# A hybrid encoder block with 16 experts: the router's sort cut into two runs of 64, stored rows without the norm's weight, and products without use behind the first gather

## Chip, cores and metric

The kernel runs on one core of one Trainium2 chip. The metric is the device time of one execution in microseconds (us), as the median of several runs. A profile of one execution, with the start, length and waits of every instruction, stands beside it. The engines go by these names: PE is TensorE (products), PEld its weight loads, DVE VectorE, ACT ScalarE, POOL GpSimd, SP SyncE (here a queue that issues DMAs).

## What is computed

One encoder layer over 1024 tokens of width 1024, all in float32. The part in question lies between the two halves of the layer: the output projection of the mixers, the router, and the first expert.

```
x = x + einsum('bsd,de->bse', mixed, w_out)          # output projection
h2 = rms_norm(x, norm_ffn_g)                         # x * rsqrt(mean(x*x) + eps) * norm_ffn_g
aff = softmax(h2 @ w_router)                         # 1024 tokens x 16 experts
g, idx = top_k(aff.T, 128)                           # each expert takes its 128 best tokens
xs = h2[idx]                                         # rows of each expert
y = (silu(xs @ w_gate) * (xs @ w_up)) @ w_down       # d_ff 2048
x = x + scatter_add(y * g, idx);  out = rms_norm(x, final_norm_g)
```

## The kernel before, in words

Products run in split precision: a float32 matrix is cut into a high part (`whi`, one ACT copy, L105) and the rest (`wlo`, one DVE subtraction, L106), and three products of 128x512 stand for one. Weights come in pieces of 128x1024 (512 KB each). `load` (L91) issues a piece's DMA on SP, `split` (L100) makes its two parts, `stream` (L118) runs splits `MSA` = 3 pieces and loads up to `ROOM` slots ahead of the piece in use. Nothing is reordered: each engine runs its instructions in the order in which the program names them, and only semaphores hold them.

**Output projection and router, L844 to L895.** For each of 8 token tiles `t` of 128 rows, `out_k` (L790) makes 6 products for each of 8 slices `k`; the last tile is made in two halves of 512 columns. The sum is added to `X2[t]` on DVE (L859, for the last tile L873 and L880). Between the products of tile t the program places the router's work for tile t-1:

- `route_a` (L798): 8 PE transposes of the rows, an ACT copy to `xT`, an ACT `Square` with a row sum into the scratch tile `h2`, `rstd_of` (L167: two DVE steps and an ACT `Sqrt`), then on POOL two products over 128x1024 (L818 by the inverse norm, L819 by the norm's weight `gfb`) and the DMA of the rows to `h2_d` (L820).
- `logits` (L824): 8 small products with the router's weights `wr`, which hold the norm's weight already.
- `route_b` (L831): softmax: a DVE maximum (L834), a DVE product (L835), ACT `Exp` (L836), and on DVE a reciprocal (L838) and a scaling (L839).

**The threshold.** An expert's 128 best tokens are those above the 128th largest of its 1024 values. `sort_steps` (L713) turns one or two tiles of values (PE, L718), copies them with a sign to `row` (L720) and sorts 128 values per expert by 16 times `max` (8 largest, L725) with `match_replace` (L729) between them. `merge_steps` (L734) joins a sorted tile with the best 128 so far: one elementwise maximum of a rising and a falling list (L743), then 7 levels of pairwise `max` and `min` (L750, L752) that sort the result again. These chains are Python generators. `bg(n)` (L767) runs the next n steps, taking the open sort and merge in turn; `BGN`, `BG7`, `T1` to `T3` say how many steps go at each place. After the last tile's softmax the sort of tile 7 starts (L888) and the loop at L889 runs all steps that are left.

**From threshold to the first expert.** `theta` (L891) is turned (L898), compared with all values (L902, L903); prefix sums by products (L905 to L917) give each chosen token its place; four DVE steps (L918 to L921) cut the values into three bfloat16 parts in `aux`. `prep(e)` (L934) builds one-hot rows `oh`, `gather(e)` (L939) gets token numbers and weights by 8 small products `pa` and issues the indirect DMA that fetches expert e's 128 rows from `h2_d` (L951). `xst(e)` (L955) turns those rows in two halves of four transposes, each with one ACT copy to `xh` (L964, 128x512) and one DVE subtraction to `xl` (L965). Then `gu` (L970) and `down` (L999) run for 16 experts with 4 quarters each; `xst(e+1)` is placed in quarters 2 and 3 of expert e (L1078, L1079). Ahead of expert 0 the order is `prep(0)`, `gather(0)`, two splits (`SA0` = 1), `xst(0)` (L1066 to L1069).

Of the kernel before, what the change touches and what calls it, by code (L numbers as in the profile page):

```python
# [8 lines left out]
F32 = mybir.dt.float32  # L9
# [3 lines left out]
AF = mybir.ActivationFunctionType  # L13
# [12 lines left out]
MSA, ROOM, ROOM0, PF0, PF1, SA0 = 3, 36, 43, 9, 15, 1  # L26
WOS = (0, 0, 0, 0, 0, 1, 2, 3)
FY = 4
BGN, BG7, T1, T2, T3 = 4, 3, 2, 2, 4
LAG = 2  # L30
FILL = (5, 2, 1, 1) + (1, 0, 1, 0) * 7 + (1, 1, 1, 1, 1)

# [9 lines left out]
def f32(ap):  # L42
    return ap.bitcast(F32)
# [3 lines left out]
def block_kernel(ctx, tc, x, wpre, wexp, cols, rows, sguw, out):  # L47
    nc = tc.nc
# [11 lines left out]
    def slot(shape, dt, name):  # L60
        return big.tile(shape, dt, name=name, tag="s", bufs=NSLOT)
# [10 lines left out]
    def psml(name, shape=(128, 512)):  # L72
        return psp.tile(list(shape), F32, name=name, tag="t", bufs=2)
# [90 lines left out]
    def bcast_row(t, lo_, n):  # L164
        nc.gpsimd.dma_start(t, bass.AP(tensor=rows.tensor, offset=rows.offset + lo_, ap=[[0, 128], [1, n]]))
# [540 lines left out]
    nc.vector.memset(affw, 0.0)  # L706
    aff = affw[:, :, 0:16]
    theta = cst.tile([16, 1], F32, name="theta")
    sgn = cst.tile([64, 1], F32, name="sgn")
    nc.vector.memset(sgn, -1.0)  # L710
    nc.vector.memset(sgn[0:32], 1.0)

    def sort_steps(t, n):  # L713


        rows_ = 16 + 32 * (n - 1)
        pt = psml("paT", (32 * n, 128))
# [4 lines left out]
        dst = srp.tile([64, 128], F32, name="srt", bufs=3)  # L722
        for r in range(16):
            yield
            nc.vector.max(dst[:rows_, 8 * r:8 * r + 8], cur[:rows_])  # L725
            if r < 15:
                yield
                nx = srp.tile([64, 128], F32, name="srw", bufs=4)
                nc.vector.match_replace(nx[:rows_], dst[:rows_, 8 * r:8 * r + 8], cur[:rows_], -3.0e38)  # L729
                cur = nx  # L730
        for j in range(n):
            SRT[t + j] = dst[32 * j:32 * j + 16]

    def merge_steps(t):  # L734

        o = SRT.pop(t)
        if t % 2 and t < 6:
            v = srp.tile([16, 128], F32, name="bit", bufs=4)
            nc.vector.tensor_copy(v, o)
            o = v  # L740
            yield
        m = srp.tile([16, 128], F32, name="bit", bufs=4)
        nc.vector.scalar_tensor_tensor(m, o, -1.0, TOP[0], op0=OP.mult, op1=OP.max)  # L743
        d = 64 if t < 7 else 0
        while d:
            nx = srp.tile([16, 128], F32, name="bit", bufs=4)
            a = m.rearrange("p (b two d) -> p b two d", two=2, d=d)
            b = nx.rearrange("p (b two d) -> p b two d", two=2, d=d)
            yield
            nc.vector.tensor_tensor(b[:, :, 0], a[:, :, 0], a[:, :, 1], op=OP.max)  # L750
            yield
            nc.vector.tensor_tensor(b[:, :, 1], a[:, :, 0], a[:, :, 1], op=OP.min)  # L752
            m = nx
            d //= 2
        TOP[0] = m

# [3 lines left out]
    def start_sort(t, n):  # L760
        g = sort_steps(t, n)
        next(g)
        SG.append(g)
# [58 lines left out]
    PL = {}  # L822

# [5 lines left out]
            mm(PL[t], xT[:, k, :], wr[:, k, :], start=(k == 0), stop=(k == 7))  # L829

    def route_b(t, n=0):  # L831
        rs = RT.pop(t)[2]
# [53 lines left out]
    logits(7, range(4, 8))  # L886
    route_b(7, T3)
    start_sort(7, 1)  # L888
    while SG or MG or merged[0] < 7:  # L889
# [28 lines left out]
    nc.vector.tensor_copy(aux[:, :, :, 2], aff)  # L918
    nc.vector.tensor_tensor(tmp, aff, aux[:, :, :, 2], op=OP.subtract)
    nc.vector.tensor_copy(aux[:, :, :, 3], tmp)  # L920
    nc.vector.tensor_tensor(aux[:, :, :, 4], tmp, aux[:, :, :, 3], op=OP.subtract)  # L921
    slotm = cst.tile([128, 8, 16], F32, name="slotm")
    sel = srp.tile([128, 8, 16], F32, name="sel")
# [31 lines left out]
    def xst(e, parts=(0, 1)):  # L955
        if parts[0] == 0:
            XT[e] = slot([128, 8, 128], F32R, "xh"), slot([128, 8, 128], F32R, "xl")
        xh, xl = XT[e]
        for j in parts:
            pt = psml("pxs", (128, 4, 128))  # L960
            for k in range(4):
                nc.tensor.transpose(pt[:, k, :], XS[e][:, (4 * j + k) * 128:(4 * j + k + 1) * 128], ident)  # L962
            js = slice(4 * j, 4 * j + 4)
# [199 lines left out]
```

## Time and profile before

| what | value |
|---|---|
| median of 3 runs | 1991.76 us (1989.69 to 1995.08) |
| the profiled execution, own time | 1993.92 us |
| its span in the trace | 1992.1 us |
| PE busy | 1892.0 us, 95% of the span |
| DVE busy | 1441.3 us, 72% |
| ACT busy | 1167.5 us, 59% |
| POOL busy | 255.9 us, 13% |
| mean granted TensorE clock | 0.978 |
| DMA, mean over the span | 258 GB/s |

Times in the trace count from the span's start. A granted clock of 1.00 is 2.4 GHz and 0.50 is 1.2 GHz. Busy shares are averages over stages with different limits, so the stage of the change is to be read by itself: the projection and router end near 817 us, the experts begin near 857 us and end near 1955 us. An engine's line in the timeline names the producer whose end finished the idle time before it.

### The profile page before, as it was taken

What the parts mean: (1) busy time and instruction counts of PE and PEld (TensorE: products, weight loads), DVE (VectorE), ACT (ScalarE), POOL (GpSimd) and SP (SyncE); (2) the same over time, 40 slices, a digit from 0 to 9 for tenths busy, and PEclk for the clock granted to TensorE, in tenths of its full rate; (3) what the DMA queues carried; (4) which work ended last, traced back from release to release, by engine and by line L of the source; (5) the groups of instructions that cost most, each with busy time, mean ns of one, the idle gap of its engine ahead of it and who ended that gap; (6) DMA issues with size and microseconds to landing.
All of it is one profiled execution on the core that took longest, in us unless ns stands there. A gap on an engine that the chain in (4) does not pass through costs nothing. (4 is left out here: it accounts for less than half of the span.)

```text
span 1992.1 us, 25890 instructions
## 1 busy us (share of the span) xinstructions
PE 1892.0 (95%) x9094; PEld 1541.4 (77%) x9094; DVE 1441.3 (72%) x1981; ACT 1167.5 (59%) x1473; POOL 255.9 (13%) x191
## 2 busy tenths in 40 slices
PE   7999999998999999489999999999999999999993
PEld 5788888876778878368888888888788878888883
DVE  5142111228886657889999989999899989899985
ACT  5232221216665334267778777777777777777774
POOL 0000000006663424200000000000000000000010
PEclk9999999999998999789999999999999999999997
DMA  5023210333212665659999999999999999999982
GB/s 215 32 74 116 95 74 31 114 103 112 75 43 92 238 253 189 264 192 327 399 369 385 375 399 370 367 391 400 364 377 383 398 365 375 388 378 388 378 327 95
DMA packets 140740, 513.64 MB, mean 258 GB/s; under 512 B 15649, under 2 KB 15665, under 8 KB 140609
## 3 DMA queue, kind: packets, MB, share of 16 engines
q1 hardware_dynamic: 127008, 462.48, 61.1%
q0 software_dynamic: 13600, 49.51, 7.6%
q8 instruction: 71, 1.16, 0.2%
q14 instruction: 61, 0.49, 0.1%
HBM read 472.08 MB, written 39.85 MB: 257 GB/s over the span
## 5 line engine op out<-in xcount | busy, mean ns | idle before, releaser
L106 DVE TENSOR_TENSOR wlo<-raw,whi 128x1024 fp32r<-128x1024 f32 x820 | 954.9, 1222 | 199.5 <-ACT whi L105 192.0
L105 ACT ACTIVATE whi<-raw 128x1024 fp32r<-128x1024 f32 x820 | 800.9, 1049 | 19.5 <-issue 17.4
L981 PE MATMUL pgu<-whi,xh 128*128 128x512 f32 x1024 | 326.8, 400 | 0.0
L981 PE MATMUL pgu<-wlo,xh 128*128 128x512 f32 x1024 | 318.0, 392 | 0.0
L981 PE MATMUL pgu<-whi,xl 128*128 128x512 f32 x1024 | 316.6, 390 | 0.0
L1011 PE MATMUL py<-whi,ht 128*128 128x512 f32 x1024 | 285.0, 390 | 1.8 <-ACT whi L105 0.9
L1011 PEld LDWEIGHTS py<-whi,ht 128*128 128x128 f32 x1024 | 191.8, 188 | 43.3 <-ACT whi L105 1.9
L981 PEld LDWEIGHTS pgu<-whi,xl 128*128 128x128 f32 x1024 | 192.7, 188 | 42.1
L981 PEld LDWEIGHTS pgu<-wlo,xh 128*128 128x128 f32 x1024 | 192.7, 188 | 41.5
L981 PEld LDWEIGHTS pgu<-whi,xh 128*128 128x128 f32 x1024 | 184.6, 189 | 32.3 <-ACT xh L964 0.3
L1011 PE MATMUL py<-wlo,ht 128*128 128x512 f32 x512 | 159.2, 392 | 1.8 <-DVE wlo L106 1.6
L951 POOL DMA_INDIRECT xs<-h_d,idx x16 | 23.0, 1439 | 879.7 <-ACT whi L105 301.2
L1011 PEld LDWEIGHTS py<-wlo,ht 128*128 128x128 f32 x512 | 95.0, 188 | 25.3 <-DVE wlo L106 6.4
L995 ACT ACTIVATE ht<-pht 128x512 fp32r<-128x512 f32 x64 | 38.3, 599 | 120.2 <-PE pht L993 120.2
L316 ACT ACTIVATE gst<-pg,colt 128x1024 f32<-128x1024 f32 x16 | 17.8, 1115 | 145.7 <-PE pg L216 137.4
L426 DVE CUSTOM_DVE_ANT_0 sc<-pS,tabs 128x1024 f32<-128x1024 f32 x64 | 78.1, 1221 | 25.4 <-PE pS L415 23.6
L432 ACT ACTIVATE sc<-sc,zz 128x1024 f32<-128x1024 f32 x64 | 73.2, 1146 | 19.1 <-DVE zz L426 14.4
L216 PE MATMUL pg<-hTh,whi 128*128 128x512 f32 x256 | 81.0, 398 | 0.0
L216 PE MATMUL pg<-hTh,wlo 128*128 128x512 f32 x256 | 80.7, 396 | 0.0
L216 PE MATMUL pg<-hTl,whi 128*128 128x512 f32 x256 | 80.7, 396 | 0.0
L983 ACT ACTIVATE hh<-pgu 128x512 f32<-128x512 f32 x64 | 38.2, 597 | 56.2 <-PE pgu L981 54.4
L445 POOL TENSOR_TENSOR sc<-sc,zz 128x768 f32<-128x768 f32 x32 | 53.4, 1668 | 80.9 <-DVE zz L437 75.2
(259 smaller groups left out, 2550.6 us busy)
## 6 DMA issues: line engine op xcount, KB each, us to landing
raw<-wexp SPq DMA_DIRECT2D x768, 512.0 KB, 7.3
raw<-wpre SPq DMA_DIRECT2D x52, 512.0 KB, 3.9
gin<-gate_d SPq DMA_DIRECT2D x24, 512.0 KB, 4.8
gate_d<-gst POOLq DMA_DIRECT2D x16, 512.0 KB, 2.9
stk_d<-st POOLq DMA_DIRECT2D x12, 512.0 KB, 3.6
ST<-stk_d POOLq DMA_DIRECT2D x12, 512.0 KB, 4.0
x<-x SPq DMA_DIRECT2D x8, 512.0 KB, 9.8
xr<-x SPq DMA_DIRECT2D x8, 512.0 KB, 6.3
```

What stands on the lines that cost most here:

```text
L105: nc.scalar.activation(h, r, AF.Copy)
L106: nc.vector.tensor_sub(l, r, f32(h))
L216: mm(p[:, n * 512:(n + 1) * 512], a[:, ks], b[:, n * 512:(n + 1) * 512], start=first, stop=last)
L316: nc.scalar.activation(g, p, AF.Sigmoid, bias=b_gate[:, b:b + 1])
L426: nc.vector.tensor_tensor_reduce(s, PR[i][c], tabs[:, 896 - qt * 128:1920 - qt * 128], -slope(h), 3.0e38, op0=OP.add, op1=OP.min, accum_ou ...
L432: nc.scalar.activation(s, s, AF.Exp, bias=ZZ[i][:, c:c + 1], scale=-1.0, accum_out=zall[:, c, i:i + 1])
L445: nc.gpsimd.tensor_tensor(p1[:, a], p1[:, a], zz[:, 3:4].to_broadcast([128, POOLC]), op=OP.mult)
L951: nc.gpsimd.indirect_dma_start(out=xs, out_offset=None, in_=h2_d[:, :], in_offset=bass.IndirectOffsetOnAxis(ap=idx[:, :1], axis=0))
L981: mm(p[:, n * 512:(n + 1) * 512], a[:, k, :], b[:, n * 512:(n + 1) * 512], start=f, stop=l)
L983: nc.scalar.activation(hh[:, 0], p[:, 0:512], AF.Silu)
L995: nc.scalar.activation(ht[:, 0], pt, AF.Copy)
L1011: mm(p[:, n * 512:(n + 1) * 512], ht[:, a, f, :], b[:, n * 512:(n + 1) * 512], start=s_, stop=l)
```

## The change

- **Sort:** the 128 values of each expert in a tile are laid out as two runs of 64 on separate partitions, one of them with its sign turned. 8 times `max` and 7 times `match_replace` sort both runs in the same instructions, now 64 wide. A copy brings the second run beside the first, two `scalar_tensor_tensor` steps form minimum and maximum, and 6 levels of pairwise `min` and `max` finish the list of 128. The list now rises; `merge_steps` has the signs to match.
- **Rows:** `gfb` and its load are gone, the two POOL products are gone. `route_b` stores `X2[t]` times the inverse norm (one ACT copy with a scale per row) and issues the row DMA. The norm's weight is applied in `xst`, where a row's channels lie on partitions: one ACT copy with a scale and one DVE step for each 128x128 block, 8 and 8 for an expert in place of 2 and 2.
- **Order:** `Square` goes ahead of the copy to `xT` in the last tile's halves too. The four `aux` steps move from behind the comparison into the loop that runs the last sort steps, which now takes two steps at a time. `sel` uses the tile `tmp`.
- **Rates:** `BGN, BG7, T1, T2, T3` go from 4, 3, 2, 2, 4 to 5, 4, 3, 3, 3.
- **Products without use:** behind `gather(0)` come `WARM` = 14 bfloat16 products of 128x512 of `ones_b` with `oh`, into a PSUM tile that nobody reads.

```
-BGN, BG7, T1, T2, T3 = 4, 3, 2, 2, 4
+BGN, BG7, T1, T2, T3 = 5, 4, 3, 3, 3
+WARM = 14
...
-    gfb = slot([128, 1024], F32, "gfb")
-    bcast_row(gfb, 1792, 1024)
...
+    def halves(m, d, first):
+        nx = srp.tile([48, 128], F32, name="bit", bufs=7)
...
+        for j, op in enumerate((first, OP.min if first == OP.max else OP.max)):
+            yield
+            nc.vector.tensor_tensor(b[:, :, j], a[:, :, 0], a[:, :, 1], op=op)
...
-        cur = srp.tile([64, 128], F32, name="row", bufs=2)
-        nc.vector.tensor_scalar(cur[:rows_], pt[:rows_], sgn[:rows_] if t == 0 else -1.0, None, op0=OP.mult)
-        yield
+        cur = srp.tile([128, 64], F32, name="row", bufs=2)
+        nc.vector.tensor_scalar(cur[:w], pt[:, 0:64], sgn[:w] if t == 0 else 1.0, None, op0=OP.mult)
+        nc.vector.tensor_scalar(cur[w:2 * w], pt[:, 64:], sgn[w:2 * w] if t == 0 else -1.0, None, op0=OP.mult)
...
-        for r in range(16):
+        for r in range(8):
             yield
             nc.vector.max(dst[:rows_, 8 * r:8 * r + 8], cur[:rows_])
-            if r < 15:
+            if r < 7:
...
+        nc.vector.tensor_copy(v[:np_], dst[w:w + np_])
+        m = srp.tile([48, 128], F32, name="bit", bufs=7)[:np_]
+        for j, op in enumerate((OP.min, OP.max)):
+            yield
+            nc.vector.scalar_tensor_tensor(m[:, 64 * j:64 * j + 64], v[:np_], -1.0, dst[:np_], op0=OP.mult, op1=op)
+        d = 32
+        while d > 1:
+            m = yield from halves(m, d, OP.min)
+            d //= 2
...
@@ route_a
-        if nh == 1:
-            nc.scalar.activation(xT[:, 4 * h0:4 * h0 + 4], pt, AF.Copy)
         nc.scalar.activation(h2[:, cs], xr[:, cs], AF.Square, accum_out=rs[:, 6 * h0:6 * h0 + 1])
-        if nh == 2:
-            nc.scalar.activation(xT, pt, AF.Copy)
+        nc.scalar.activation(xT[:, 4 * h0:4 * h0 + 4 * nh], pt, AF.Copy)
...
-            nc.gpsimd.tensor_tensor(h2, xr, rs[:, 1:2].to_broadcast([128, 1024]), op=OP.mult)
-            nc.gpsimd.tensor_tensor(h2, h2, gfb, op=OP.mult)
-            nc.gpsimd.dma_start(h2_d[t * 128:t * 128 + 128, :], h2)
@@ route_b, behind the Exp and ahead of bg(n)
+        nc.scalar.activation(h2, X2[t], AF.Copy, scale=rs[:, 1:2])
+        nc.gpsimd.dma_start(h2_d[t * 128:t * 128 + 128, :], h2)
@@ the loop of the last steps; the four steps of AUX are L918 to L921
     while SG or MG or merged[0] < 7:
-        bg(1)
+        bg(2)
+        if AUX:
+            AUX.pop(0)()
@@ xst
-            nc.scalar.activation(xh[:, js], pt, AF.Copy)
-            nc.vector.tensor_sub(xl[:, js], pt, f32(xh[:, js]))
+            for k in range(4):
+                d = 4 * j + k
+                g = g_ffn[:, d:d + 1]
+                nc.scalar.activation(xh[:, d], pt[:, k], AF.Copy, scale=g)
+                nc.vector.scalar_tensor_tensor(xl[:, d], pt[:, k], g, f32(xh[:, d]), op0=OP.mult, op1=OP.subtract)
@@ ahead of expert 0
     prep(0)
+    OH0 = OH[0]
     gather(0)
+    pw = psml("pw")
+    for j in range(WARM):
+        mm(pw, ones_b, OH0[:, 4 * (j % 2):4 * (j % 2) + 4, :], start=True, stop=True)
     stream(NPRE, SA0, ROOM0)
     xst(0)
```

## Rows read from the trace of the kernel before

**Rows 1.** Windows by stage: length; busy PE, PEld, DVE, ACT, POOL; clock, DMA share, GB/s.

```profile
800.00:816.40 16.40, 15.20 (x82) 12.24 (x80) 15.01 (x67) 8.10 (x13) 5.40 (x4) 1.00 0.34 129
827.15:844.30 17.15, 0.40 (x2) 0.15 (x2) 16.37 (x106) 0.00 (x0) 0.00 (x0) 0.50 1.02 412
844.30:849.57 5.27, 2.59 (x33) 2.41 (x33) 4.12 (x11) 0.00 (x0) 0.00 (x0) 0.50 0.03 12
855.55:871.00 15.45, 15.41 (x65) 12.54 (x66) 13.17 (x16) 11.34 (x12) 1.50 (x1) 0.79 0.01 2
871.00:1955.40 1084.40, 1081.77 (x5031) 888.94 (x5031) 992.69 (x984) 829.34 (x930) 49.05 (x30) 1.00 0.98 371
```

**Rows 2.** Waits of PE while the experts run: us in total, times, longest.

```profile
PE py L1011 <- DVE wlo L106: 1.6, 3, 0.5
```

**Rows 3.** Timeline of PE ahead of expert 0: start, us, instruction, idle before and releaser.

```profile
855.59 1.94 PE L962 MATMUL pxs<-ident,xs 128*128 128x128 f32 x8 [6.03 <-DMA xs<-h_d,idx]
857.42 1.22 PE L981 MATMUL pgu<-whi,xh 128*128 128x512 f32 x2
```

**Rows 4.** Timeline of DVE, the chain from the last sum to the prefix sums.

```profile
818.27 0.67 DVE L880 TENSOR_TENSOR xr<-xr,po 128x512 f32<-128x512 f32 x1
...
821.00 0.16 DVE L815 TENSOR_TENSOR rs<-rs 128x1 f32<-128x1 f32 x1 [1.66 <-ACT h L811]
...
823.95 2.30 DVE L752 TENSOR_TENSOR bit<-bit 16x64 f32<-16x64 f32 x1
...
827.59 0.28 DVE L720 TENSOR_SCALAR row<-paT 16x128 f32<-16x128 f32 x1 [0.56 <-PE paT L718]
...
843.85 0.28 DVE L891 TENSOR_REDUCE theta<-bit 16x1 f32<-16x128 f32 x1
...
846.93 0.29 DVE L925 SCALAR_TENSOR_TENSOR sel<-pc,eq 128x128 f32<-128x128 f32 x1 [0.24 <-PE pc L908]
```

**Rows 5.** Line L835: least, median and longest duration in ns, first and last start.

```profile
L835 DVE SCALAR_TENSOR_TENSOR rs<-rs x8: 159/850/1733, 726.7 to 822.0; 128x1 f32<-128x1 f32 x8
```

**Rows 6.** Line L819, the second POOL product, in the same columns.

```profile
L819 POOL TENSOR_TENSOR h<-h,gfb x8: 2351/2374/2400, 723.7 to 823.8; 128x1024 f32<-128x1024 f32 x8
```

**Rows 7.** Timeline of DVE: two sorts side by side, then a merge alone.

```profile
832.90 0.46 DVE L725 MAX8 srt<-srw 16x8 f32<-16x128 f32 x2
...
838.34 0.47 DVE L725 MAX8 srt<-srw 16x8 f32<-16x128 f32 x2
...
842.77 0.21 DVE L750 TENSOR_TENSOR bit<-bit 16x64 f32<-16x64 f32 x1
842.92 0.21 DVE L752 TENSOR_TENSOR bit<-bit 16x64 f32<-16x64 f32 x1
843.16 0.21 DVE L750 TENSOR_TENSOR bit<-bit 16x64 f32<-16x64 f32 x1
```

**Rows 8.** Timeline of POOL: the issue of the first gather.

```profile
850.80 1.44 POOL L951 DMA_INDIRECT xs<-h_d,idx  x1 [23.75 <-DVE ax L949]
```

**Rows 9.** Line L951, all 16 gathers: us from issue to landing.

```profile
DMA to landing us min/median/max: 4.7/8.1/9.7
```

**Rows 10.** Timeline of PE: the end of a wait in the first projection tile.

```profile
708.19 1.14 PE L795 MATMUL po<-wlo,mh 128*128 128x512 f32 x2 [3.48 <-DVE wlo L106]
```

**Rows 11.** Windows of half a microsecond, columns as in the first group.

```profile
711.50:712.00 0.50, 0.50 (x3) 0.36 (x3) 0.50 (x1) 0.00 (x0) 0.00 (x0) 0.77 1.14 434
861.50:862.00 0.50, 0.50 (x3) 0.41 (x2) 0.50 (x2) 0.00 (x0) 0.00 (x0) 0.59 0.00 0
```

**Rows 12.** Lines L964, L196, L653 and L965: copies of turned blocks, durations in ns.

```profile
L964 ACT ACTIVATE xh<-pxs x32: 597/599/600, 856.8 to 1872.9; 128x512 fp32r<-128x512 f32 x32
...
L196 ACT ACTIVATE hTh<-pT,colt x16: 679/688/694, 13.6 to 46.0; 128x512 fp32r<-128x512 f32 x16
...
L653 ACT ACTIVATE mh<-gin x64: 292/294/312, 672.8 to 706.8; 128x128 fp32r<-128x128 f32 x64
...
L965 DVE TENSOR_TENSOR xl<-pxs,xh x32: 682/691/693, 857.4 to 1873.5; 128x512 fp32r<-128x512 f32 x32
```

More of the change, by code (lines that the diff above doesn't have):

```diff
@@ L708, in block_kernel @@
     theta = cst.tile([16, 1], F32, name="theta")
-    sgn = cst.tile([64, 1], F32, name="sgn")
-    nc.vector.memset(sgn, -1.0)
-    nc.vector.memset(sgn[0:32], 1.0)
+    sgn = cst.tile([128, 1], F32, name="sgn")
+    nc.vector.memset(sgn, 1.0)
+    nc.vector.memset(sgn[0:32], -1.0)
+    nc.vector.memset(sgn[96:128], -1.0)
+    def halves(m, d, first):
+        nx = srp.tile([48, 128], F32, name="bit", bufs=7)
+        np_ = m.shape[0]
+        a = m.rearrange("p (b two d) -> p b two d", two=2, d=d)
+        b = nx[:np_].rearrange("p (b two d) -> p b two d", two=2, d=d)
+        for j, op in enumerate((first, OP.min if first == OP.max else OP.max)):
+            yield
+            nc.vector.tensor_tensor(b[:, :, j], a[:, :, 0], a[:, :, 1], op=op)
+        return nx[:np_]
@@ L713, in sort_steps @@
     def sort_steps(t, n):
-        rows_ = 16 + 32 * (n - 1)
-        pt = psml("paT", (32 * n, 128))
+        w = 32 * n
+        pt = psml("paT", (w, 128))
         nc.tensor.transpose(pt, affw[:, t:t + n, :].rearrange("p t e -> p (t e)"), ident)
-        cur = srp.tile([64, 128], F32, name="row", bufs=2)
-        nc.vector.tensor_scalar(cur[:rows_], pt[:rows_], sgn[:rows_] if t == 0 else -1.0, None, op0=OP.mult)
-        yield
-        dst = srp.tile([64, 128], F32, name="srt", bufs=3)
-        for r in range(16):
+        cur = srp.tile([128, 64], F32, name="row", bufs=2)
@@ L724, in sort_steps @@
+        nc.vector.tensor_scalar(cur[:w], pt[:, 0:64], sgn[:w] if t == 0 else 1.0, None, op0=OP.mult)
+        nc.vector.tensor_scalar(cur[w:2 * w], pt[:, 64:], sgn[w:2 * w] if t == 0 else -1.0, None, op0=OP.mult)
+        pt = None
+        rows_ = 2 * w - 16
+        dst = srp.tile([128, 64], F32, name="srt", bufs=2)
+        for r in range(8):
             yield
             nc.vector.max(dst[:rows_, 8 * r:8 * r + 8], cur[:rows_])
-            if r < 15:
+            if r < 7:
                 yield
-                nx = srp.tile([64, 128], F32, name="srw", bufs=4)
+                nx = srp.tile([128, 64], F32, name="srw", bufs=3)
@@ L729, in sort_steps @@
                 nc.vector.match_replace(nx[:rows_], dst[:rows_, 8 * r:8 * r + 8], cur[:rows_], -3.0e38)
                 cur = nx
+        yield
+        np_ = w - 16
+        v = srp.tile([48, 64], F32, name="run", bufs=1)
+        nc.vector.tensor_copy(v[:np_], dst[w:w + np_])
+        m = srp.tile([48, 128], F32, name="bit", bufs=7)[:np_]
+        for j, op in enumerate((OP.min, OP.max)):
+            yield
+            nc.vector.scalar_tensor_tensor(m[:, 64 * j:64 * j + 64], v[:np_], -1.0, dst[:np_], op0=OP.mult, op1=op)
@@ L731, in sort_steps @@
+        d = 32
+        while d > 1:
+            m = yield from halves(m, d, OP.min)
+            d //= 2
+        o = srp.tile([48, 128], F32, name="srd", bufs=3)[:np_]
+        a = m.rearrange("p (b two) -> p b two", two=2)
+        b = o.rearrange("p (b two) -> p b two", two=2)
+        for j, op in enumerate((OP.min, OP.max)):
+            yield
+            nc.vector.tensor_tensor(b[:, :, j], a[:, :, 0], a[:, :, 1], op=op)
         for j in range(n):
-            SRT[t + j] = dst[32 * j:32 * j + 16]
+            SRT[t + j] = o[32 * j:32 * j + 16]
@@ L737, in merge_steps @@
         if t % 2 and t < 6:
-            v = srp.tile([16, 128], F32, name="bit", bufs=4)
+            v = srp.tile([16, 128], F32, name="odd", bufs=1)
             nc.vector.tensor_copy(v, o)
@@ L741, in merge_steps @@
             yield
-        m = srp.tile([16, 128], F32, name="bit", bufs=4)
-        nc.vector.scalar_tensor_tensor(m, o, -1.0, TOP[0], op0=OP.mult, op1=OP.max)
+        m = srp.tile([48, 128], F32, name="bit", bufs=7)[:16]
+        nc.vector.scalar_tensor_tensor(m, TOP[0], -1.0 if t == 1 else 1.0, o, op0=OP.mult, op1=OP.max)
         d = 64 if t < 7 else 0
         while d:
[L746 to L753, printed above, removed]
+            m = yield from halves(m, d, OP.max)
             d //= 2
@@ L831, in route_b @@
     def route_b(t, n=0):
-        rs = RT.pop(t)[2]
+        _, h2, rs = RT.pop(t)
         pl = PL.pop(t)
@@ L888, in block_kernel @@
     start_sort(7, 1)
+    AUX = [lambda: nc.vector.tensor_copy(aux[:, :, :, 2], aff),
+           lambda: nc.vector.tensor_tensor(tmp, aff, aux[:, :, :, 2], op=OP.subtract),
+           lambda: nc.vector.tensor_copy(aux[:, :, :, 3], tmp),
+           lambda: nc.vector.tensor_tensor(aux[:, :, :, 4], tmp, aux[:, :, :, 3], op=OP.subtract)]
     while SG or MG or merged[0] < 7:
-        bg(1)
+        bg(2)
+        if AUX:
+            AUX.pop(0)()
     nc.vector.tensor_reduce(theta, TOP[0], axis=AX.X, op=OP.min)
@@ L917, in block_kernel @@
     prefix(pc, eq, True, False)
[L918 to L921, printed above, removed]
     slotm = cst.tile([128, 8, 16], F32, name="slotm")
-    sel = srp.tile([128, 8, 16], F32, name="sel")
+    sel = tmp
     nc.vector.tensor_tensor(slotm, pg, gt, op=OP.mult)
@@ L1066, in block_kernel @@
     prep(0)
+    OH0 = OH[0]
     gather(0)
+    pw = psml("pw")
+    for j in range(WARM):
+        mm(pw, ones_b, OH0[:, 4 * (j % 2):4 * (j % 2) + 4, :], start=True, stop=True)
+    pw = OH0 = None
     stream(NPRE, SA0, ROOM0)
```

1 line of the change is left out of this document (removed).

## Prediction

> **What bounds the kernel now.** I read the busy time by stage first. While the experts run, PE is busy for 1081.8 of 1084.4 us [rows 1], so it idles 2.6 us, and the view of waits puts 1.6 us of that down to a low part that was late [rows 2]. That stage is bound by PE, and the change removes no product from it. Ahead of it lies a hole. The projection ends near 816.4 us with PE busy 15.2 of 16.4 us; from 827.15 to 844.3 us PE has 0.4 us of work and DVE 16.37 us [rows 1]; the first rows of expert 0 reach PE at 855.59 us, after 6.03 us of waiting for the gather, and the first product starts at 857.42 us [rows 3]. Nothing else runs on PE, so each microsecond taken out of this chain comes off the end, as long as the experts' stage keeps its length.
>
> I then walked the chain on the DVE timeline [rows 4]. It starts with the last sum (818.27 us), goes through softmax to the values of tile 7 being copied for the sort (827.59 us), and through the remaining steps of the sorts to `theta` (843.85 us). That is 9.32 and 16.26 us. The first gather leaves 7 us behind `theta`.
>
> **Step 1, from the last sum to the start of sort 7.** Two DVE steps in this chain are drawn out while POOL multiplies: L835 takes 1.73 us at 822.0 us where its fastest of eight is 0.16 us [rows 5], and the merge step at 823.95 us takes 2.30 us [rows 4], just after the second POOL product, 2.4 us long, began at 823.8 us [rows 6]; the same step takes 0.21 us later [rows 7]. The POOL products go, so 1.57 + 2.09 = 3.7 us go. For the first part the square root must come earlier as well, since its table change would otherwise be late next: L815 waited 1.66 us for `Square` [rows 4], which stood behind the copy to `xT`; with `Square` first it starts when the sum ends (818.27 + 0.67 us) and not behind the turn and the copy, by my estimate 1.1 us sooner. Added in this chain: the ACT copy that makes the stored row stands behind the `Exp` and nothing of the chain behind it on ACT; the row's DMA has some 15 us until the gather. Both cost nothing; their cover is the tail of the sort.
>
> The last sum itself came late because DVE had 15.0 of 16.4 us of work [rows 1]. Per slot 4 steps run in place of 3, each cheaper. Counted through, the steps of sorts 4 and 6 and merges 4 and 5 ahead of that sum come to about the same time as before. I take 0, with 1.5 us to either side. In the earlier tiles the 5 steps per slot run beside products, and the sorts are done before the next tile's transposes are due: 0. The load of `gfb` that goes had no reader waiting: 0.
>
> **Step 2, the tail of the sort.** I followed `bg` step by step. Before, 78 steps are left when sort 7 starts: 27 `max`, 26 `match_replace`, 23 pairwise, 2 joins. Two sorts side by side take 5.44 us for 24 steps from 832.90 to 838.34 us, 0.227 us each [rows 7]; 53 of them make 12.0 us, and the other 25 then share 4.2 us, 0.17 us each. After, 55 steps and the 4 of `aux` are left: 8 `max` and 7 `match_replace` of 64 columns, 35 pairwise, 2 forming minimum and maximum, a copy, 2 joins. A 64-wide sort step is not in the trace. It lies between 0.15 us, the distance of two pairwise steps on 64 columns (842.77 to 842.92 us), and an unchanged 0.227 us. I take 0.16 us, near the lower end, for it reads the same 64 columns. Of the pairwise steps 27 have another chain beside them, 0.15 us each; the last 8 stand alone, where a level of two takes 0.39 us (842.77 to 843.16 us) [rows 7]. So: 15 x 0.16 = 2.4; 27 x 0.15 = 4.05; 4 x 0.39 = 1.6; 5 others at 0.25 = 1.25; the second `row` copy 0.25; 4 `aux` steps at 0.29, the length of L925 [rows 4], 1.2. The sum is 10.7 us against 16.26 us: **5.5 us less**. With every sort step at 0.227 and every pairwise one at 0.195 us it is 13.2 us, 3.1 us less; with all 64-wide steps at 0.13 us and the `aux` steps in gaps 7 us less.
>
> **Step 3, `aux`.** It leaves the chain behind `theta`, but there DVE waited 0.24 us for PE's sums at 846.93 us [rows 4]; PE is the later one. So its removal there gains 0, and its 1.2 us in step 2 are a loss.
>
> **Step 4, the gather.** It will be issued about 9 us sooner, near 841.5 us. Before, DMA ran at 412 GB/s with a share of 1.02 until about 844.3 us and then at 12 GB/s [rows 1], so the first gather of 850.80 us [rows 8] met idle engines and landed after 4.7 us, the least of all 16; the median, beside full prefetch, is 8.1 us [rows 9]. The prefetch depends on slots and bandwidth and not on this chain, so the new gather overlaps its last 3 us or so. The loss lies between 0 and 3.4 us; I take 1.0, since most of its time lies behind the prefetch's end. The Trainium skill (DMA: Bandwidth & Descriptors, Queues, rings and completion order) says that each DMA engine takes turns between its queues packet by packet; by that, an estimate, the gather's 512 KB would go at half of 412 GB/s for its whole length and lose 1.3 us, and the total would be 0.3 us worse. No row before shows a first gather under load.
>
> **Step 5, the products without use.** They stand on PE between the 8 products of `gather(0)` and the transposes, where PE waited 6.03 us [rows 3]. PE's 5031 instructions among the experts, most of 512 columns, take 1081.8 us at the full clock, 0.215 us each [rows 1]; at the half clock 14 of them take 14 x 0.43 = 6.0 us, or about 5 if the clock rises on the way. After the wait that ended at 708.19 us [rows 10] it was half and rose near 711.7 us, 3.5 us into the products; at expert 0 it rose near 861.9 us [rows 11], 4.5 us into them. So it should be full when the rows land. Gain: the transposes took 1.83 us [rows 3] and would take 0.9; the 4.5 us of products at the half clock would take 2.3 us. Against it, only two pieces are split ahead; at the full clock PE asks for the third 1.5 us sooner than before, while DVE is at 13.2 of 15.45 us [rows 1]. I put 1.0 us of that as given back. Net 0.9 + 2.2 - 1.0 = 2.1, say **2.0 us less**, between 0.2 us less (no rise) and 3.0.
>
> **Step 6, `xst` in 16 pieces.** ACT's copy of 128x512 takes 0.60 us, with a scale per partition 0.69 us, and a 128x128 one 0.29 us; DVE's step on 512 columns 0.69 us [rows 12]. Eight small ones with a scale run at most 0.3 us apart, 2.4 against 1.2 us: up to 1.2 us more on ACT per expert, and on DVE, at up to 0.25 us a step, up to 0.6 us. What hides it: three pieces of lookahead, 4 us of products, and 92 us of idle DVE time over 15 experts [rows 1]. If that cover is gone it is the third rival. I take 0.
>
> **Sum.** -3.7 - 5.5 + 0 + 1.0 - 2.0 + 0 = -10.2 us. The profiled execution took 1993.9 us, so 1983.7 us. The median of the runs shown is 2.2 us below it, so against the median the forecast is **1981.5 us**.
>
> **Rivals.** *The gather lands late and the clock falls back.* If it takes 8.1 us, PE idles some 3.5 us behind the 14 products, as long as the 3.48 us after which it came back at the half clock [rows 10, 11]. Then step 4 costs 3.4 and step 5 gains 0.2: -6.0 us, 1985.7. For it: DMA is full up to 844.3 us. Against: the prefetch ends then.
>
> *A step costs the same whatever its width.* The tail gains 3.1 us, the total is -7.8 us, 1983.9. For it: two dependent 64-wide steps stand further apart, 843.16 against 842.92 us, than two free ones. Against: side by side the steps pack at 0.15 us [rows 7].
>
> *The split holds PE up in each expert (slower).* Place: the ACT and DVE queues in quarters 2 and 3, where splits stand behind the turned blocks. Price: 1.2 + 0.6 = 1.8 us for each of 15 experts, 27 us, so +16.8 us, 2008.6. It decides from 0.7 us of new PE wait per expert. For it: PE has waited for splits. Against: all PE idle time of that stage is 2.6 us, 1.6 us of it behind a split [rows 1, 2]. The Trainium skill (ScalarE: Activation LUTs, What ACT_TABLE_LOAD costs) puts an ACTIVATE at 186 ns + 0.833 ns per column, 93 ns more for a pointer operand, with 93 ns of overlap in a row; by that, an estimate, ACT has 1.3 us more per expert, and the trace agrees on 128 columns (293 against 294 ns) and on the scale (93 against 89 ns). It speaks against this part of the change, but only if ACT's queue is late.
>
> **Chances.** A measurement of this kernel tells about 0.3%, 6.0 us, from no change. Forecast 0.63; late gather 0.18 (half of it within 6 us); width without effect 0.11; held up 0.05; other mishaps of a few us, a later last sum among them, 0.03. So faster 0.80, same 0.14, slower 0.06. The best of all bounds, -15.2 us, gives 1976.5; the worst without the third rival, with the last sum 1.5 us late and the tail 3.1 us shorter, -2.1 us, 1989.7. Leaving out 2 in 10: 1976 to 1988.5.
>
> **What will show it.** `theta` near 834.6 us; L835 at 0.16 us each time and no POOL product of 1024 columns beside the router; from sort 7's first copy to `theta` 10 to 11 us; the first gather's landing between 4.7 and 8.1 us; the clock at 1.00 under the first expert products, and how long PE waits for the third piece; PE's waits from the first expert's end on no longer than 3 us. I am wrong if the experts' stage grows, or if `theta` comes less than 7 us sooner.

## The result, and the profile after

The changed kernel takes 2023.19 us (median of 4 runs, 2020.85 to 2023.89), the kernel before 1991.85 us beside it: 1.0154 times as long, 95% interval 1.014 to 1.0167. The forecast was 1981.5 us and faster. The experts' stage grew, which the prediction named as a sign of being wrong.

The page of the profile, part 1 (busy us, share of the span, instructions), kernel after:

```profile
span 2022.0 us, 26013 instructions
...
PE 1917.0 (95%) x9108; PEld 1536.8 (76%) x9108; DVE 1433.9 (71%) x2038; ACT 1200.0 (59%) x1577; POOL 221.2 (11%) x174
```

The router first. Timeline of DVE, kernel after, beside [rows 4], and two lines in the columns of [rows 5] and [rows 9]:

```profile
818.75 0.67 DVE L901 TENSOR_TENSOR xr<-xr,po 128x512 f32<-128x512 f32 x1
...
823.48 0.16 DVE L853 SCALAR_TENSOR_TENSOR rs<-rs 128x1 f32<-128x1 f32 x1
...
825.16 0.21 DVE L731 TENSOR_SCALAR row<-paT 32x64 f32<-32x64 f32 x1 [0.56 <-PE paT L729]
...
835.21 0.27 DVE L918 TENSOR_REDUCE theta<-bit 16x1 f32<-16x128 f32 x1
...
838.28 0.29 DVE L948 SCALAR_TENSOR_TENSOR auxt<-pc,eq 128x128 f32<-128x128 f32 x1 [1.05 <-PE pc L935]
```

```profile
L853 DVE SCALAR_TENSOR_TENSOR rs<-rs x8: 159/160/161, 727.2 to 823.5; 128x1 f32<-128x1 f32 x8
```

```profile
DMA to landing us min/median/max: 4.6/8.0/9.2
```

The chain from the last sum to the first copy for sort 7 went from 9.32 to 6.41 us, the tail from there to `theta` from 16.26 to 10.05 us. PE reaches the rows of expert 0 at 846.93 us, where it was 855.59 us [rows 3]: 8.66 us sooner. The last sum itself came 0.48 us later; that says little, since with the same code up to it it lies anywhere from 813.86 to 818.75 us in the traces of the changed kernel and its variants. Timeline of PE, kernel after:

```profile
840.78 5.46 PE L1097 MATMUL pw<-oh,ones_b 128*128 128x512 bf16 x14
846.93 1.07 PE L985 MATMUL pxs<-ident,xs 128*128 128x128 f32 x8 [0.70 <-DMA xs<-h_d,idx]
848.07 0.73 PE L1006 MATMUL pgu<-whi,xh 128*128 128x512 f32 x2
...
850.47 0.61 PE L1006 MATMUL pgu<-whi,xl 128*128 128x512 f32 x2
853.98 0.73 PE L1006 MATMUL pgu<-whi,xh 128*128 128x512 f32 x2 [2.90 <-ACT whi L106]
855.24 0.90 PE L1006 MATMUL pgu<-wlo,xh 128*128 128x512 f32 x2 [0.52 <-DVE wlo L107]
```

The first 12 products (two pieces of weights) run at the full clock; then PE waits 2.9 us for the third piece's high part. Then the experts. Windows, kernel after, columns as in [rows 1], first around expert 0, then from the first to the last turn of a hidden block (`pht`):

```profile
846.90:851.00 4.10, 4.00 (x20) 3.04 (x20) 1.65 (x5) 1.73 (x5) 0.00 (x0) 1.00 0.00 0
851.00:854.00 3.00, 0.10 (x2) 0.02 (x1) 1.10 (x5) 2.12 (x5) 0.00 (x0) 1.00 0.00 0
854.00:860.00 6.00, 5.48 (x16) 4.08 (x17) 6.00 (x6) 5.09 (x6) 0.00 (x0) 0.72 0.01 4
870.50:1985.50 1115.00, 1096.22 (x5009) 877.91 (x5007) 1001.88 (x1069) 847.29 (x1015) 49.09 (x30) 1.00 0.96 360
```

The same stretch of the kernel before:

```profile
876.30:1955.50 1079.20, 1076.57 (x5008) 884.72 (x5007) 988.28 (x979) 824.95 (x925) 49.05 (x30) 1.00 0.98 371
```

It grew from 1079.2 to 1115.0 us, 35.8 us; ahead of it, from the first transpose of expert 0's rows to the first `pht`, 20.7 became 23.6 us. So -8.7 + 2.9 + 35.8 = +30.0 us, against 2022.0 - 1992.1 = 29.9 us of span. The products and the clock are the same; DVE has 13.6 us more work and ACT 22.3 us more in 1115 us, so neither is full. PE's busy time grew by 19.65 us for the same products, so about half of the 35.8 us stands inside it and not as idle time. Waits in that stretch, kernel after, beside [rows 2] (us in total, times, longest):

```profile
ACT xh L989 <- DVE xl L990: 52.0, 90, 1.2
DVE xl L990 <- ACT xh L989: 39.2, 90, 0.4
...
PEld py L1036 <- DVE wlo L107: 25.9, 45, 1.0
PEld pgu L1006 <- DVE wlo L107: 18.6, 30, 1.0
...
PE py L1036 <- DVE wlo L107: 10.1, 20, 0.5
PE pgu L1006 <- DVE wlo L107: 7.9, 15, 0.5
```

PE now waits 18.0 us for low parts, its weight loads 44.5 us. One wait stands there that the kernel before does not have, that of ACT's pieces of the turned rows for DVE's; that of DVE's for ACT's was 9.4 us there, 15 times, and is 39.2 us now, 90 times. Timeline of DVE in one half of a block of rows, kernel after, whose transposes began at 1175.70 us:

```profile
1176.98 0.34 DVE L990 SCALAR_TENSOR_TENSOR xl<-pxs,colt,xh 128x128 fp32r<-128x128 f32 x1
1177.76 0.35 DVE L990 SCALAR_TENSOR_TENSOR xl<-pxs,colt,xh 128x128 fp32r<-128x128 f32 x1 [0.43 <-ACT xh L989]
1178.54 0.35 DVE L990 SCALAR_TENSOR_TENSOR xl<-pxs,colt,xh 128x128 fp32r<-128x128 f32 x1 [0.43 <-ACT xh L989]
1179.33 0.35 DVE L990 SCALAR_TENSOR_TENSOR xl<-pxs,colt,xh 128x128 fp32r<-128x128 f32 x1 [0.44 <-ACT xh L989]
1180.27 2.36 DVE L107 TENSOR_TENSOR wlo<-raw,whi 128x1024 fp32r<-128x1024 f32 x2 [0.59 <-ACT whi L106]
```

The same half in the kernel before, whose transposes began at 1171.34 us:

```profile
1172.62 0.69 DVE L965 TENSOR_TENSOR xl<-pxs,xh 128x512 fp32r<-128x512 f32 x1
1173.55 2.36 DVE L106 TENSOR_TENSOR wlo<-raw,whi 128x1024 fp32r<-128x1024 f32 x2 [0.24 <-ACT whi L105]
```

A pair of pieces repeats every 0.78 us, though each lasts 0.35 to 0.37 us: while one engine works the other stands. The next low part starts 4.57 us after the transposes, before 2.21 us.

### The profile page after: what moved, and what is told of

It is laid out like the page before. It is cut to its first block, busy times and chain, and to the rows that moved or that the text cites. A ratio compares the mean times of both kernels' runs of the same rounds, so it can differ in the third digit from the quotient of the medians.

```text
span 2022.0 us, 26013 instructions
## 1 busy us (share of the span) xinstructions
PE 1917.0 (95%) x9108; PEld 1536.8 (76%) x9108; DVE 1433.9 (71%) x2038; ACT 1200.0 (59%) x1577; POOL 221.2 (11%) x174
## 5 line engine op out<-in xcount | busy, mean ns | idle before, releaser
L1006 PEld LDWEIGHTS pgu<-wlo,xh 128*128 128x128 f32 x1024 | 190.1, 188 | 58.7 <-DVE wlo L107 19.5
L1006 PEld LDWEIGHTS pgu<-whi,xh 128*128 128x128 f32 x1024 | 183.3, 189 | 39.6 <-ACT whi L106 8.1
L1036 PE MATMUL py<-wlo,ht 128*128 128x512 f32 x512 | 163.1, 400 | 10.2 <-DVE wlo L107 10.1
L989 ACT ACTIVATE xh<-pxs,colt 128x128 fp32r<-128x128 f32 x128 | 46.9, 367 | 108.1 <-DVE xl L990 54.5
L317 ACT ACTIVATE gst<-pg,colt 128x1024 f32<-128x1024 f32 x16 | 17.8, 1115 | 145.6 <-PE pg L217 137.4
L1020 ACT ACTIVATE ht<-pht 128x512 fp32r<-128x512 f32 x64 | 38.1, 596 | 109.7 <-PE pht L1018 109.7
L990 DVE SCALAR_TENSOR_TENSOR xl<-pxs,colt,xh 128x128 fp32r<-128x128 f32 x128 | 44.6, 349 | 46.0 <-ACT xh L989 46.0
```

What stands on the lines that cost most here:

```text
L317: nc.scalar.activation(g, p, AF.Sigmoid, bias=b_gate[:, b:b + 1])
L989: nc.scalar.activation(xh[:, d], pt[:, k], AF.Copy, scale=g)
L990: nc.vector.scalar_tensor_tensor(xl[:, d], pt[:, k], g, f32(xh[:, d]), op0=OP.mult, op1=OP.subtract)
L1006: mm(p[:, n * 512:(n + 1) * 512], a[:, k, :], b[:, n * 512:(n + 1) * 512], start=f, stop=l)
L1020: nc.scalar.activation(ht[:, 0], pt, AF.Copy)
L1036: mm(p[:, n * 512:(n + 1) * 512], ht[:, a, f, :], b[:, n * 512:(n + 1) * 512], start=s_, stop=l)
```

## The experiments

The theory is that this taking of turns, 4 x 0.785 us a half and 6.3 us an expert in both queues, is the loss. Head is the time from the first transpose of expert 0's rows to the first `pht`, stage from there to the last `pht`, by first and last start of these lines in each trace, that is, in the one execution that was profiled; the time is the median of all runs. The expectations call head and stage together the stage: 1138 us after and 1100 us before. Absolute times are not compared: with equal code up to there, sort 7's first `max` began at 828.5 us in the profile before and at 824.2 us in that of "before, four ahead".

| kernel | head us | stage us | time us | ratio to before (95%) |
|---|---|---|---|---|
| before | 20.7 | 1079.2 | 1991.85 | |
| after: turns, 3 pieces of lookahead | 23.6 | 1115.0 | 2023.19 | 1.014 to 1.0167 |
| the change to `xst` alone | 23.0 | 1113.3 | 2022.95 | 1.013 to 1.0171 |
| grouped | 19.6 | 1080.9 | 1983.59 | 0.9936 to 0.9969 |
| one step per engine, no weight | 18.3 | 1080.7 | 1981.72 | 0.993 to 0.9964 |
| one half grouped | 21.7 | 1089.7 | 1991.92 | 0.9989 to 1.001 |
| turns, own tiles | 23.7 | 1119.2 | 2026.66 | 1.0148 to 1.0185 |
| turns, DVE off the PSUM block | 19.5 | 1080.8 | 1983.20 | 0.9939 to 0.9969 |
| turns, 4 pieces | 23.3 | 1090.0 | 1999.69 | 1.0029 to 1.0062 |
| turns, 5 pieces | 23.6 | 1073.2 | 1978.78 | 0.9914 to 0.9952 |
| before, 5 pieces | 20.6 | 1073.3 | 1985.47 | 0.9956 to 0.9979 |
| grouped, no products | 20.0 | 1078.9 | 1982.67 | 0.9933 to 0.996 |
| grouped, four ahead | 18.1 | 1076.9 | 1979.93 | 0.9919 to 0.9947 |
| grouped, four ahead, no products | 19.6 | 1076.5 | 1979.17 | 0.9921 to 0.9948 |
| grouped, four ahead, `aux` late | 18.1 | 1076.2 | 1979.45 | 0.9918 to 0.9948 |
| before, four ahead | 19.1 | 1076.0 | 1987.42 | 0.9969 to 0.9987 |
| grouped, four ahead, 5 pieces | 18.1 | 1073.3 | 1975.61 | 0.9903 to 0.9935 |

**Which part of the change.** The part alone, in the kernel before:

```
-    gfb = slot([128, 1024], F32, "gfb")
-    bcast_row(gfb, 1792, 1024)
...
-            nc.gpsimd.tensor_tensor(h2, h2, gfb, op=OP.mult)
...
-            nc.scalar.activation(xh[:, js], pt, AF.Copy)
-            nc.vector.tensor_sub(xl[:, js], pt, f32(xh[:, js]))
+            for k in range(4):
...
+                nc.scalar.activation(xh[:, d], pt[:, k], AF.Copy, scale=g)
+                nc.vector.scalar_tensor_tensor(xl[:, d], pt[:, k], g, f32(xh[:, d]), op0=OP.mult, op1=OP.subtract)
```

> The kernel before with one part of the change alone: the rows stored without the norm's weight, which the turned rows then take in 16 pieces that take turns between ScalarE and VectorE. Theory (this part is the whole loss): the last sum and the sort stay as before within 4 us, the stage of the experts takes about 1138 us in place of 1100, the time is 2025 to 2032 us. Rival (the loss needs the early start, the products without use or the new sort): under 2005 us.

It took 2022.95 us, head and stage together 1136.3 us, 36.4 us more than before. The time is 2 us under the theory's range, since `theta` came at 835.8 us where it was 843.9 us; the part has one POOL product less beside the router as well. The loss is in this part, whatever the sort and the products do.

**Turns or small pieces.** The same 16 pieces in another order:

```
             for k in range(4):
                 d = 4 * j + k
-                g = g_ffn[:, d:d + 1]
-                nc.scalar.activation(xh[:, d], pt[:, k], AF.Copy, scale=g)
-                nc.vector.scalar_tensor_tensor(xl[:, d], pt[:, k], g, f32(xh[:, d]), op0=OP.mult, op1=OP.subtract)
+                nc.scalar.activation(xh[:, d], pt[:, k], AF.Copy, scale=g_ffn[:, d:d + 1])
+            for k in range(4):
+                d = 4 * j + k
+                nc.vector.scalar_tensor_tensor(xl[:, d], pt[:, k], g_ffn[:, d:d + 1], f32(xh[:, d]), op0=OP.mult, op1=OP.subtract)
```

> The changed kernel, with the same 16 pieces of the turned rows' split, but per half the four of ScalarE first and then the four of VectorE, in place of taking turns. Theory (each piece waits for the other engine's piece before it, so both queues stand for 6.3 us per expert and the experts' stage is 38.5 us longer): the waits go, the stage from the landing of the gathered rows to the last product of the weights' heads falls from 1138 to about 1100 us, and the time to 1982 to 1986 us. Rival (the number of small operations itself fills the two queues): the stage stays above 1125 us and the time above 2010 us.

And the old two steps per half, which leave the norm's weight out, so that this kernel computes something else:

```
-            for k in range(4):
-                d = 4 * j + k
-                g = g_ffn[:, d:d + 1]
-                nc.scalar.activation(xh[:, d], pt[:, k], AF.Copy, scale=g)
-                nc.vector.scalar_tensor_tensor(xl[:, d], pt[:, k], g, f32(xh[:, d]), op0=OP.mult, op1=OP.subtract)
+            js = slice(4 * j, 4 * j + 4)
+            nc.scalar.activation(xh[:, js], pt, AF.Copy)
+            nc.vector.tensor_sub(xl[:, js], pt, f32(xh[:, js]))
```

> The changed kernel with the old split of the turned rows, one operation of ScalarE and one of VectorE per half; the norm's weight is left out of the rows that the experts get. Theory of the taking of turns: the stage is 1100 us, the time 1981 to 1984 us, and within 4 us of the grouped pieces. Rival (small operations cost by themselves): this one is 1981 to 1984 us too, but the grouped pieces stay 25 us or more behind it.

Grouped: 1983.59 us, stage 1080.9 us. The view of ACT's pieces in the grouped kernel (durations in ns, then idle us and times):

```profile
L988 ACT ACTIVATE xh<-pxs,colt x128: 360/368/410, 845.5 to 1863.1; 128x128 fp32r<-128x128 f32 x128
...
its engine sat idle before it (us, times) until:
  PE pxs L985: 63.4, 31
```

The wait for DVE is gone and the pieces are as long as with turns; the work of ACT and DVE in the stage is nearly the same (839.35 and 997.99 us, with turns 847.29 and 1001.88). Timeline of DVE in the same half of a block of rows, grouped, whose transposes began at 1160.83 us:

```profile
1162.64 1.12 DVE L991 SCALAR_TENSOR_TENSOR xl<-pxs,colt,xh 128x128 fp32r<-128x128 f32 x4 [0.45 <-ACT xh L988]
1163.68 2.35 DVE L107 TENSOR_TENSOR wlo<-raw,whi 128x1024 fp32r<-128x1024 f32 x2
```

Four pieces of one engine in a row start 0.25 to 0.26 us apart. The next low part starts 2.85 us after the transposes, with turns 4.57 and before the change 2.21 us. With two steps the time is 1981.72 us: smallness and the weight together cost 1.9 us, which lies inside the spread of those runs (1979.64 to 1983.58), the order 39.6 us.

**How much of it the queues bear.** The first half grouped, the second taking turns:

```
+            if j == 0:
+                (the two grouped loops)
+            else:
+                (the loop that takes turns)
```

> The changed kernel with the pieces of the first half of the turned rows grouped and those of the second half taking turns. Theory: each half costs its 3.1 us of standing queues, so about half of the loss is left, the stage at 1115 to 1125 us and the time at 1998 to 2010 us. Rival (the queues have slack for one half's waits and none for the second's): under 1992 us.

1991.92 us, 8.3 us over the grouped kernel. The loss is neither halved, as the theory had it, nor gone; the time lies under the rival's bound by 0.08 us alone, well inside the spread (1989.32 to 1995.67). One half's turns cost 8.3 us and the second's 31.3 us more, so most of one half's standing is covered.

**Why they take turns.** In the first kernel the high pieces have tiles of their own, so that ACT never writes a tile that DVE reads; in the second DVE reads only the high pieces, so that its low parts are not those of the rows:

```
-NSLOT = 32
+NSLOT = 30
...
-            XT[e] = slot([128, 8, 128], F32R, "xh"), slot([128, 8, 128], F32R, "xl")
+            XT[e] = [own.tile([128, 128], F32R, name=f"xh{d}", bufs=2) for d in range(8)], slot([128, 8, 128], F32R, "xl")
...
```

> The changed kernel, its pieces still taking turns, but each of the eight high pieces in a tile of its own (two slots fewer in the pool for that). Theory A (the two engines are made to take turns because both read one PSUM block): nothing changes, ScalarE still waits for VectorE 96 times for some 54 us, and the time stays at 2015 to 2030 us. Theory B (they take turns because ScalarE writes, and VectorE reads, one tile of high pieces): the waits of ScalarE go and the time is 1983 to 1992 us.

```
-                nc.vector.scalar_tensor_tensor(xl[:, d], pt[:, k], g, f32(xh[:, d]), op0=OP.mult, op1=OP.subtract)
+                nc.vector.scalar_tensor_tensor(xl[:, d], f32(xh[:, d]), g, f32(xh[:, d]), op0=OP.mult, op1=OP.subtract)
```

> The changed kernel, its 16 pieces taking turns in the same order, but VectorE's pieces read only the tile of high pieces and not the PSUM block (so the low parts that it stores are not the low parts of the rows). Theory A (one PSUM block read by two engines makes them take turns): ScalarE no longer waits for VectorE, the stage is back at 1100 us and the time is 1981 to 1987 us. Theory B (the order of issue, or the tile of high pieces): the time stays above 2010 us.

The same view, first kernel:

```profile
L990 ACT ACTIVATE xh<-pxs,colt x128: 361/367/370, 845.0 to 1904.9; 128x128 fp32r<-128x128 f32 x128
its engine sat idle before it (us, times) until:
  PE pxs L986: 55.0, 31
  DVE xl L991: 53.7, 96
```

and second:

```profile
L989 ACT ACTIVATE xh<-pxs,colt x128: 359/368/413, 845.3 to 1863.1; 128x128 fp32r<-128x128 f32 x128
...
its engine sat idle before it (us, times) until:
  PE pxs L985: 63.3, 31
```

The first still takes turns, 2026.66 us; the second does not, 1983.20 us. ACT waits because DVE reads the same PSUM block (4 pieces of 128 columns in one tile), though each reads other columns and neither writes it. The Trainium skill (PSUM — Partial Sum Buffer, PSUM bank collisions raise a hardware error) says of the compiler back end's scheduler that it sets a dependency between any two instructions on different engines that touch the same bank and the same 32 partitions, reads and writes alike, and that colliding accesses raise an error. The two runs agree with such a dependency; how reads without the wait would do was not tried.

**What should have covered it.** `MSA` is the number of pieces that are split ahead among the experts.

```
-MSA, ROOM, ROOM0, PF0, PF1, SA0 = 3, 36, 43, 9, 15, 1
+MSA, ROOM, ROOM0, PF0, PF1, SA0 = 5, 36, 43, 9, 15, 1
```

> The changed kernel, its pieces taking turns, with weights split five pieces ahead in place of three. Theory (both queues stand for 6.3 us in each expert, and three pieces of lookahead, 4 us of products, cover it only in part): with five pieces, 6.9 us of products, most of the loss goes and the time is 1985 to 2000 us. Rival (the queues have no time left to get five pieces ahead between two experts): the time stays within 5 us of 2023 us.

And with four:

```
+MSA, ROOM, ROOM0, PF0, PF1, SA0 = 4, 36, 43, 9, 15, 1
```

> The changed kernel, its pieces taking turns, with weights split four pieces ahead in place of three. Theory (the loss is what both queues stand in an expert, 6.3 us, less what the lookahead covers, 4 us with three pieces, 5.5 with four, 6.9 with five, times 15): 0.8 x 15 = 12 us above the kernel with five, 1988 to 1995 us. Rival (three pieces are a threshold, above which nothing is lost): 1977 to 1982 us.

And the line with five in the kernel before:

> The kernel before with five pieces of lookahead among the experts in place of three, and nothing else. Theory (before, PE waited 2.6 us in that stage, so there is next to nothing to cover): 1988 to 1994 us. Rival (the lookahead itself is worth time): below 1985 us.

Waits of ACT's pieces among the experts, turns with five pieces, where no wait of PE for a split is left (the window of that stage has PE busy in all of its 1073.20 us):

```profile
ACT xh L989 <- DVE xl L990: 69.7, 90, 2.3
```

```profile
866.00:1939.20 1073.20, 1073.20 (x5008) 886.09 (x5007) 998.98 (x1070) 844.63 (x1014) 57.47 (x30) 1.00 0.98 374
```

The turns stand there as before, even longer, and cost nothing. By single experts, from the first `pht` of one to that of the next (median of 15): 68.49 us in the kernel before and in the grouped one, with three pieces and with five; with turns 70.84, 69.45 and 68.49 us with three, four and five pieces. So the turns cost 2.35, 0.96 and 0 us an expert. The queues' 6.3 us less 4.1, 5.5 and 6.9 us of cover (1.37 us of products a piece) make 2.2, 0.8 and 0. That fits these three, but the sum is bookkeeping: for one half's turns, 3.1 us, it gives no loss, and an expert of that kernel takes 69.09 us, 0.6 us more.

More lookahead is worth something without turns, too, and more than I expected: the stage is 1080.9 us grouped and 1079.2 us before with three pieces, and 1073.3 us in both with five. In the kernel before this lies in six of the experts, which take 68.8 to 70.6 us. Early in each of the six ACT pauses for 2.3 to 4.0 us ahead of a high part, and the view of waits names no releaser:

```profile
ACT whi L105 <- issue: 17.4, 6, 4.0
```

With five pieces no such row is left. Why ACT pauses there is open. My three ranges missed to either side, since they left out that worth: 1978.78 us lies under 1985, 1999.69 above 1995, and the kernel before with five, 1985.47 us, between theory and rival.

**The products without use.** The grouped kernel without them:

```
-WARM = 14
+WARM = 0
```

> The changed kernel with grouped pieces and without the products that have no use behind the first gather. Theory of the forecast (they keep the clock up, worth 2.0 us net, at most 3.0): the first transposes and products of expert 0 run at the half clock, and the time is 1.5 to 3 us above the grouped kernel, 1985 to 1987 us. Rival (what the clock gives, the third piece's split gives back): within 1 us of the grouped kernel, 1983 to 1984.6 us.

The grouped kernel with four pieces split ahead of expert 0, and then both edits:

```
-MSA, ROOM, ROOM0, PF0, PF1, SA0 = 3, 36, 43, 9, 15, 1
+MSA, ROOM, ROOM0, PF0, PF1, SA0 = 3, 36, 43, 9, 15, 3
```

> The changed kernel with grouped pieces and with four pieces of the weights of expert 0 split ahead of the first turned rows in place of two. Theory (at the full clock the products of expert 0 wait for the third and the following split): the two waits of 0.36 us at 850 and 853 us go, the time falls by 0.7 to 1.5 us to 1982 to 1983 us. Rival (the splits stand in front of the first turned rows on ScalarE and VectorE): the same or 1 to 2 us more.

> The changed kernel with grouped pieces and four pieces split ahead, without the products that have no use. Theory (their gain was given back by the third piece's split, and four pieces ahead set it free): from the landing of the first rows to the first transposed heads of expert 0 it takes 1.5 to 2.5 us longer than with them (18.1 us), and the time is 1981 to 1983 us. Rival (they are worth nothing): within 0.7 us of the kernel with them, 1979 to 1980.6 us.

Timeline of PE, grouped, no products, to be read beside that of the kernel after:

```profile
843.03 1.94 PE L985 MATMUL pxs<-ident,xs 128*128 128x128 f32 x8 [6.19 <-DMA xs<-h_d,idx]
844.63 1.22 PE L1007 MATMUL pgu<-whi,xh 128*128 128x512 f32 x2
845.64 0.80 PE L1007 MATMUL pgu<-wlo,xh 128*128 128x512 f32 x2
```

Without them the eight transposes take 1.94 us and not 1.07, as before the change (the granted clock is 0.50 in the window from 843 to 844 us); yet the head is only 0.4 us longer (20.0 against 19.6), with four pieces ahead 1.5 us (19.6 against 18.1), and neither kernel's time shows it (0.9 and 0.8 us the other way, inside the spread). With four pieces ahead PE waits for no split in the head; with two it waits 0.7 us with the products and 0.4 us without. So I read it thus: what the clock gives, the late splits take, with two pieces ahead nearly all. The four pieces themselves gave 3.7 us (1983.59 to 1979.93), where 0.7 to 1.5 were expected, and they do so without the change, too, where I expected nothing. The same line (`SA0` from 1 to 3) in the kernel before:

> The kernel before, with four pieces of the weights of expert 0 split ahead of its first turned rows in place of two and nothing else. Theory (before, the half clock gave the splits time, so there was nothing to gain): 1992 to 1994 us, the ratio within 0.1 per cent of 1. Rival (the pieces ahead are worth 3 to 4 us whatever else is changed): 1988 to 1990.5 us.

1987.42 us, 5.8 us under the kernel before beside it: 1.6 us in the head, 3.2 us in the stage. In the stage four of ACT's six pauses are gone and two are left, 6.2 us together; why is open.

**The four `aux` steps**, back behind the prefix sums (with grouped pieces and four ahead):

```
         bg(2)
-        if AUX:
-            AUX.pop(0)()
...
     prefix(pc, eq, True, False)
+    for f in AUX:
+        f()
```

> The changed kernel with grouped pieces and four pieces split ahead, with the four steps on the affinities' parts back behind the prefix sums, where they stood before. Theory of the forecast (they cost 1.2 us in the tail of the sort and cover nothing behind it): from the second row copy of sort 7 to theta 8.5 to 9.3 us in place of 10.05 us, 0.3 to 1 us back before the first gather, and the time 1978.5 to 1980 us. Rival (they lay in gaps of the sort): theta as early as with them, and the issue of the first gather up to 1.2 us later.

From sort 7's first copy to `theta` 9.25 us, with them 10.05 us; from there to the issue of the first gather 16.2 and 17.0 us. The steps cost 0.8 us, all of which reaches the gather; the time, 1979.45 against 1979.93 us, is too coarse to tell it.

**The version to keep** has grouped pieces, four pieces ahead of expert 0 and five among the experts:

```
+MSA, ROOM, ROOM0, PF0, PF1, SA0 = 5, 36, 43, 9, 15, 3
```

> The changed kernel with grouped pieces, five pieces of lookahead among the experts and four pieces split ahead of expert 0. Theory (with the turns gone there is nothing left for more lookahead to cover; four pieces ahead of expert 0 give 3.7 us): 1976 to 1981 us, within 3 us of the kernel with three pieces and four ahead. Rival (the lookahead itself is worth time in the experts' stage): 1965 to 1974 us.

1975.61 us (6 runs), ratio 0.9919 with an interval of 0.9903 to 0.9935, faster than both kernels. The stage, 1073.3 us, has what five pieces give it; the time lies just under the theory's range and above the rival's, since lookahead was worth 3.6 us in the stage.

## Why the prediction was wrong, step by step

- **Step 1** was right in its cause: the POOL products' stretching is gone (L853 at 0.16 us all eight times, [rows 5]). The chain gained 2.9 us of the 3.7 foretold. It overlooked that with `Square` first the copy to `xT` comes later, and with it the logits: their products start 2.53 us after the last sum, before 2.07, and DVE waits 1.85 us for them.
- **Step 2** was right: the tail gained 6.2 us, 5.5 foretold. It holds the `aux` steps, 0.8 us by the experiment and not 1.2. The terms of its dear end add up to 12.9 us and not 13.2, which moves that bound by 0.3 us and nothing else.
- **Step 3** was right: nothing is gained behind `theta`, where DVE waits 1.05 us for PE.
- **Step 4** was too dear by its 1.0 us: from `theta` to the first transposes it is 11.72 us after and 11.74 before, and the least landing 4.6 us. DMA still ran at 397 GB/s while the gather was being issued, up to 843 us, but the gather's own rows moved from 844 us on. So the Trainium skill's rule on queues that take turns (DMA: Bandwidth & Descriptors, Queues, rings and completion order) could not be seen here.
- **Step 5**'s mechanism was right, its give-back too small: full clock under the first products, as foretold, but 0.4 us in the head of the grouped kernel, not 2.0. In the changed kernel itself the head is 2.9 us longer, for the turns hold the third piece back and the clock falls with the wait (0.72 in the window from 854 us).
- **Step 6 failed**, and it alone turned the sign. "Eight small ones with a scale run at most 0.3 us apart" took each engine's steps by themselves: that holds for the pieces of one engine in a row (0.25 us apart, grouped). In the order of the change they are 0.367 and 0.350 us long, and 0.785 us apart, since each waits for the other engine. "What hides it: three pieces of lookahead, 4 us of products, and 92 us of idle DVE time" set an idle sum over 15 experts against a wait inside a queue that runs in order: 6.3 us of standing in each expert against 4 us of cover. The term taken as 0 measured 38.1 us against the grouped pieces.
- **The third rival** had the place right (splits behind the turned blocks, PE waiting for low parts) and the mechanism half: it priced 1.8 us of added work per expert, where grouped pieces show that added work costs 1.9 us in all. The wait between engines costs 34 us in the stage and 4 us in the head. The durations were not what misled. The Trainium skill's formula for an ACTIVATE (ScalarE: Activation LUTs, What ACT_TABLE_LOAD costs) gives, as an estimate, 386 ns for 128 columns with a scale; the trace has 367 ns.

Without the turns the sum comes close: grouped, the change takes 1983.59 us, 9.5 us less than before beside it, where -10.2 us was foretold. By terms, with the chain as in the kernel after, it is -2.9 (foretold -3.7), -6.2 (-5.5), 0 (+1.0), -1.1 in the head (-2.0) and +1.7 us in the stage (0), -8.5 us together; the rest lies inside the spread. The errors go to either side and nearly cancel, so that so small a difference is in part luck.

## What to carry to other kernels

When one step is cut into pieces on two engines, ask for every piece what it waits for on the other engine, and which PSUM block both read: with all pieces of one engine first and then all of the other the next split came 0.6 us later here in each half than with two large steps, with turns 2.4 us later. Set such a standing time against the lookahead at that place (pieces ahead times the time of a piece), and not against an engine's idle sum. Where a loss is a late split, try a longer lookahead also by itself.

## What was not expected of the hardware and the program

- ACT and DVE reading different columns of one PSUM block follow one another in this program: 0.367 + 0.350 us of work in each 0.785 us, so a handover costs about 0.03 us each way; the price is the lost overlap, of the two engines and of one engine's pieces in a row.
- Five pieces of lookahead in place of three are worth 5.6 us in the kernel before (1985.47 against 1991.04 us beside it, interval of the ratio 0.9956 to 0.9979), where PE was idle for only 2.6 us of that stage [rows 1]. The window above puts PE at 1076.57 us busy there; with five pieces and the same products it is 1073.30 us: part of what stood as busy was waiting that the record does not show as idle.
